# A third token tile of 128 rows in a one-core hybrid layer (mLSTM, SSD, ConvFFN), FFN constant rows read at another time, and another order of the first transfers

## The chip, the core and the metric

The kernel runs on one core of one Trainium2 chip. The metric is the device time of one execution in microseconds (us); the kernel before is given as three runs with their median, and one further execution was profiled. Engines are called by the profile's names: PE (matmul), PEld (its weight load), DVE, ACT, POOL and SP. SP issues nearly all of the transfers; POOL and ACT issue some.

## What is computed

One layer of a decoder, in f32, for 256 prompt tokens (one sequence, states start at zero) and 64 sample tokens (8 sequences of 8 tokens, each with states of its own):

```
u = x @ w_in                                   # 2048 -> q, k, v, o, gates, z, xbc, dt
h_m = mLSTM(q, k, v, gates)                    # 4 heads of 256; per sequence a carried C, n, m
h_s = SSD(z, conv4(xbc), dt)                   # 16 heads of 64, 2 groups; per sequence a carried S
x1 = LN1(alpha * x + [h_m, h_s] @ w_out)
up = x1 @ w_up                                 # 2048 -> 2 * 5504
c = conv3(up) ; f = (silu(c_g) * c_v) @ w_down
y = LN2(alpha * x1 + f)
```

Within a sequence of L tokens both mixers are a masked L x L product (the scores with their decays, times v) plus a carry-in: the state at the sequence's start, seen through q or C. The outputs are y for both token sets and every new state.

## The kernel before, in words

**Tokens and weights.** The 320 tokens (NT) lie in the free dimension of all large products: a bank holds 128 outputs x 320 tokens. f32 is kept by splitting both sides: x into XH and XL (rounded part and rest), each weight tile into hi and lo. Each tile of 128 x 128 weights takes three matmuls of 320 columns (XH·hi, XL·hi, XH·lo); there are 9456 of these, called main matmuls here. Class `Stream` brings the weights: raw blocks by DMA into a ring of 4 (L61), a quarter of 128 x 512 at a time rounded by ACT to hi (L74) and subtracted by DVE to lo (L75), into rings of 5.

**Stages.** w_in; w_out; then up and down projection in three parts; at the end LN2 (L1618 to L1661). `run_groups` (L262) walks through the weight groups. L232 is the helper that records every matmul, L238 the one for every transpose.

**The rest of the work** is written as generators: `yield n` puts the next piece n units later on a clock that the program keeps for itself while it is built, and pieces are put between main matmuls when they are due on it. So the yields fix, at build time, the order of each engine's instructions; each engine then works through its own order and waits for its inputs.

**Token tiles.** Where tokens must stand in partitions, they are taken as three tiles, two of 128 prompt tokens and one of the 64 samples (`tok(i)`: 128, 128, 64). That third tile gives matmuls and transposes with 64 rows:
- `x_transpose` (L402): x comes in as [tokens, features] and is transposed on PE, three transposes per 128 features, the third from a 64-row tile; ACT writes XH (L413), DVE XL (L414).
- `load_small` (L462): the constants; the SSD conv history is [24, 1536] and takes 12 transposes.
- `ssd_sample` makes the SSD carry-in `yi` of the samples, two tiles of [128, 512] per group in which each sequence has a block of 32 partitions (8 of them used). `ssd_heads` then adds, per pair of heads, masked products for the prompt and the samples; the carry-in comes in by two matmuls with `sel`, a constant that picks the used rows. In the same bank `po` is the prompt's state update.
- `ml_chunks` makes the mLSTM carry-in: per head two tiles of [128, 257], copied from PSUM by ACT (L1176). `ml_out` waits for both and for the products of the head, and for the samples adds one masked product (64 rows) and two matmuls with `sel` of 257 columns; num is then transposed with a 64-row third piece.
- `ssd_cb`, `ml_scores`, `colbc`, `ssd_norm`, `ln1`, `down_task` and the end treat the third tile likewise, with 64 rows or 64 columns.

**Around w_out.** In this stage `out_task` (L1373) follows each of 16 outputs of 128 x 320: DVE adds alpha·x (L1376) and takes a mean off (L1389), ACT rounds it (L1391), DVE takes the rest (L1393), ACT squares (L1402), and POOL adds both into running sums s1 (L1400) and s2 (L1403). For the first output POOL copies s1 instead (helper L193). Nobody waits for the sums before LN1. `ffn_consts` (L1339) runs beside it: after `yield 25000` POOL issues 8 transfers of `state_ffn_conv` rows (L1343), one of `ffn_conv_w` (L1345) and one of `ffn_conv_b` (L1346) into tiles called rows; after `yield 20000` PE transposes the four blocks of w and b, and DVE copies them to fcol (L1351); more transposes follow for the history (hist, L1357). The up projection needs them after LN1.

**Start.** PE runs 7 matmuls on ones. SP issues x_prompt's first columns, ident (the identity that transposes need), x_sample's first columns and more; ACT's queue issues the first two w_in blocks. POOL issues the small constants.

Of the kernel before, what the change touches and what calls it, by code (L numbers as in the profile page):

```python
# [13 lines left out]
NT = 320  # L14
# [7 lines left out]
class Stream:  # L22
# [21 lines left out]
    def load(self, upto=None, own=()):  # L44

        own = list(own)
        while self.nr < len(self.raws) and (own or self.live < self.RB):
# [12 lines left out]
            for c in range(0, m, step):  # L60
                (self.nc.sync if self.nr > 1 else self.nc.scalar).dma_start(t[:, :, c:c + step], src[:, :, c:c + step])  # L61
# [109 lines left out]
def _hybrid_step(ctx, tc, I, O):  # L171
# [77 lines left out]
    def tok(i):  # L249
        return 128 if i < 2 else 64  # L250
# [3 lines left out]
    sel = cp.tile([128, 2, 64], F32, name="sel")  # L254
# [58 lines left out]
    def diag3(dg, cols_of):  # L313
        for i in range(3):
            n = tok(i)
            V.tensor_scalar(dg[0:n, i, 0:n], ident[0:n, 0:n], cols_of(i)[0:n], None, ALU.mult)
        return dg

    def colbc(dg):

        ps = bank()
        for i in range(3):
            n = tok(i)
            mm(ps[:, 128 * i:128 * i + n], ones[0:n, :], dg[0:n, i, 0:n], True, True)
        return ps
# [63 lines left out]
    for _ in range(7):  # L389
# [12 lines left out]
    def x_transpose(c, kks=range(4)):  # L402
# [4 lines left out]
        for kk in kks:  # L407
# [27 lines left out]
    xs_in = mt("T10", [64, D])  # L435
    for c in range(4):
        x_load(c)
        s = slice(512 * c, 512 * c + 512)
        dma(xs_in[:, s], I["x_sample"].rearrange("b t f -> (b t) f")[:, s])
        if c == 0:  # L440
            src = I["x_prompt"][0, :, 256:512].rearrange("(i p) f -> p i f", p=128)
            dma(box["x", 0][:, :, 256:512], src)
            own = [mt("T4", [128, 1024]) for _ in range(4)]
        st.load(2 * c + 2, (own[0:2], own[2:4], (), ())[c])
# [16 lines left out]

    def load_small():  # L462
# [14 lines left out]
        hr = mt("T10", [24, 1536])  # L477
        gdma(hr, I["state_ssm_conv"][0].rearrange("b r c -> (b r) c"))
        gdma(c_tm, I["c_tm"])
        gdma(dsk, I["ssm_D"].broadcast_to([128, 16]))  # L480
        gdma(m01, I["c_m01"])
        gdma(sel, I["c_sel"])
# [5 lines left out]
        for i in range(12):  # L488
            transpose(ps[:, 24 * i:24 * i + 24], hr[:, 128 * i:128 * i + 128])
        A.activation(histx, ps[:, 0:288].rearrange("p (a b) -> p a b", b=24), AF.Copy)  # L490
# [20 lines left out]
    def gate_task(pg):  # L511
        gf, gi = mt("T2", [128, 384]), mt("T2", [4, NT])
        V.memset(gf[:, NT:384], 0.0)
        V.tensor_copy(gf[:, 0:NT], pg[:, 0:NT])
# [5 lines left out]
        for i in range(3):  # L520
            mm(pt[:, 24 * i:24 * i + 24], gf[:, 128 * i:128 * i + 128], fold[:, 0:24], True, True)
        pf = bank()
        mm(pf[0:4, 0:NT], fold[:, 0:4], gf[:, 0:NT], True, True)
# [36 lines left out]
        transpose(pd[0:48, 0:64], dt3[0:64, 2, :])  # L560
# [4 lines left out]
        V.tensor_copy(dtf[32:48], pd[32:48, 0:64])  # L565
# [47 lines left out]
        for i in range(3):  # L613
            transpose(p1[:, 128 * i:128 * i + 128], T1[:, 128 * i:128 * i + 128])
        A.activation(TT1, p1[:, 0:384].rearrange("p (a b) -> p a b", b=128), AF.Copy)
        p2 = bank()
# [59 lines left out]
    def ssd_cb():  # L676
# [4 lines left out]
        for g in range(2):  # L681
# [3 lines left out]
            mm(ps[0:64, 384:448], B[:, g, 256:NT], C[:, g, 256:NT], True, True)  # L685
            t = mt("T2", [128, 448])
            G.memset(t[64:128, 384:448], 0.0)
            V.tensor_tensor(t[:, 0:384], ps[:, 0:384], m01[:, 0:384], ALU.mult)
            V.tensor_tensor(t[0:64, 384:448], ps[0:64, 384:448], m01[0:64, 384:448], ALU.mult)
# [76 lines left out]
    def ssd_xdt():  # L766
# [3 lines left out]
        for i in range(3):  # L770
            n = tok(i)
            for hh in range(2):
                ps = bank()
                for j in range(4):
                    transpose(ps[0:n, 128 * j:128 * j + 128], XS[:, 4 * hh + j, 128 * i:128 * i + n])
                V.tensor_tensor(by(xdt[0:n, i, 512 * hh:512 * hh + 512], 64), by(ps[0:n, :], 64),
                                bcl(dt3[0:n, i, 32 + 8 * hh:40 + 8 * hh], 64), ALU.mult)
                yield 500
        box["xdt"] = xdt
        flags.add("xdt")  # L780

    def ssd_sample():
# [22 lines left out]
        yield from wait("x4")  # L805
        yi = {}
        for b in range(8):
# [19 lines left out]
            if b % 4 == 3:  # L827
                x = b // 4
                for g in range(2):
# [6 lines left out]
                    yi[g, x] = y  # L836
# [5 lines left out]
        box["yi"] = yi  # L842
# [5 lines left out]
    def ssd_heads():  # L848
# [41 lines left out]
        for j in range(8):  # L890
# [47 lines left out]
    def ssd_norm():  # L938
        var = sm([128, 3, 2])
        G.memset(var, 1.0)  # L940
        for g in range(2):
# [10 lines left out]
            for i in range(3):  # L952
                mm(ps[0:tok(i), 2 * i:2 * i + 2], sq[:, 128 * i:128 * i + tok(i)], ones[:, 0:2], True, True)
            pv = ps[:, 0:6].rearrange("p (a b) -> p a b", b=2)
            V.tensor_scalar(var[:, 0:2, g], pv[:, 0:2, 0], 1.0 / 512, None, ALU.mult)
            V.tensor_scalar(var[0:64, 2:3, g], ps[0:64, 4:5], 1.0 / 512, None, ALU.mult)
# [769 lines left out]
```

## Time and profile before

| what | value |
| --- | --- |
| three runs, median (lowest to highest) | 1579.27 us (1578.6 to 1581.3) |
| the profiled execution: its own time, its span | 1580.12 us, 1578.3 us |
| mean clock of PE in it, share of full | 0.992 |
| PE busy, share of the span | 98% |
| DVE, ACT, POOL busy | 62%, 49%, 18% |
| HBM traffic | 231.63 MB read, 20.43 MB written |

The span runs from the first to the last instruction of the profile; the execution's own time is 1.8 us longer. In rows of the timeline the first number is the start in us from the span's start, the second the length of the (merged) row, then engine, line, operation, output<-inputs by tile name, shape and count; in brackets the idle time ahead of it and what ended it. Matmuls overlap in the pipeline, so the price of one is read from start to start, not from its length. A row of the windows gives the stretch, its length, busy time and instruction count of PE, PEld, DVE, ACT and POOL, the granted clock, the busy share of the DMA engines and GB/s.

### The profile page before, as it was taken

The page shows a single profiled execution, that of the slowest core. Times are in us where ns is not written, and L with a number is a line of the kernel's source. Part 1 is how long each engine was busy: PE and PEld are TensorE (multiplying, and loading weights), DVE is VectorE, ACT ScalarE, POOL GpSimd, SP SyncE. Part 2 cuts the span into 40 slices and gives each one's busy share as a digit, 9 for nine tenths or more (in the row PEclk, how much of TensorE's full clock was granted, in tenths as well). Part 3 has the DMA queues.
Part 4 walks back from the last instruction along what each step waited for, and adds up shares of the span by engine and source line. Part 5 has one row for each costly group of instructions (what it writes and reads, how often), then busy time and mean ns, then how long its engine had stood idle before and what let it go on. Part 6 is the DMA issues. An engine that isn't in the chain of part 4 may idle for free.

```text
span 1578.3 us, 27987 instructions
## 1 busy us (share of the span) xinstructions
PE 1553.8 (98%) x10547; PEld 1502.5 (95%) x10547; DVE 976.6 (62%) x1957; ACT 773.1 (49%) x1532; POOL 290.3 (18%) x601
## 2 busy tenths in 40 slices
PE   9999999999999997999999999999999999999997
PEld 7999999998889997999999999999999999999996
DVE  5775445656677585687777545565644465556765
ACT  3665433435445453476666435555533455555332
POOL 4213220024311073133321000000000000001301
PEclk9999999999999998999999999999999999999998
DMA  9456665577665566445554455455444545455642
GB/s 260 147 161 160 187 187 172 143 193 208 195 221 183 169 183 138 134 147 149 149 151 135 157 158 146 148 156 152 136 152 144 167 145 151 143 154 168 170 140 79
DMA packets 267080, 253.97 MB, mean 161 GB/s; under 512 B 18804, under 2 KB 261263, under 8 KB 266816
## 3 DMA queue, kind: packets, MB, share of 16 engines
q1 hardware_dynamic: 260432, 246.76, 53.2%
q0 software_dynamic: 4928, 4.37, 1.3%
q8 instruction: 82, 1.34, 0.3%
q10 hardware_dynamic: 1584, 1.05, 0.3%
q14 instruction: 54, 0.44, 0.1%
HBM read 231.63 MB, written 20.43 MB: 160 GB/s over the span
## 4 chain that ended last, share of the span: by engine, by line
PE 86%; issue 7%; DMA 2%; POOL 1%; DVE 1%; ACT 1%; POOLq 0%; SPq 0%; DVEq 0%; ACTq 0%
PE bk L232 84%; PE bk L238 2%; DMA rows<-ffn_conv_w 1%; POOL T L425 1%; DMA raw<-w_out 1%; DVE lo L75 1%; DMA T<-ln_g 0%; DMA gbias<-ssm_dt_bias 0%; DMA xT<-T 0%; POOL big L1654 0%; ACT hi L74 0%; DVE big L1393 0%; DVE big L1389 0%; ACT L657 0%; ACT T L644 0%
## 5 line engine op out<-in xcount | busy, mean ns | idle before, releaser
L75 DVE TENSOR_TENSOR lo<-raw,hi 128x512 fp32r<-128x512 f32 (+2 forms) x800 | 556.4, 706 | 391.7 <-ACT hi L74 389.3
L74 ACT ACTIVATE hi<-raw 128x512 fp32r<-128x512 f32 (+2 forms) x800 | 486.3, 616 | 455.9 <-PE bk L232 427.3
L232 PE MATMUL bk<-big,hi 128*128 128x320 f32 (+1 forms) x2752 | 609.3, 310 | 0.0
L232 PEld LDWEIGHTS bk<-big,hi 128*128 128x128 f32 x2752 | 462.2, 188 | 0.1
L232 PE MATMUL bk<-big,lo 128*128 128x320 f32 (+1 forms) x1376 | 426.5, 310 | 0.0
L232 PE MATMUL bk<-XH,hi 128*128 128x320 f32 x832 | 270.2, 325 | 0.1
L232 PEld LDWEIGHTS bk<-big,lo 128*128 128x128 f32 x1376 | 259.3, 188 | 0.0
L232 PE MATMUL bk<-XH,lo 128*128 128x320 f32 x832 | 258.2, 310 | 0.1
L232 PE MATMUL bk<-XL,hi 128*128 128x320 f32 x832 | 258.0, 310 | 0.0
L232 PE MATMUL bk<-HH,hi 128*128 128x320 f32 x688 | 214.2, 311 | 0.0
L232 PE MATMUL bk<-HH,lo 128*128 128x320 f32 x688 | 212.6, 309 | 0.0
L232 PE MATMUL bk<-HL,hi 128*128 128x320 f32 x688 | 212.5, 309 | 0.0
L232 PEld LDWEIGHTS bk<-XH,hi 128*128 128x128 f32 x832 | 157.2, 189 | 14.7 <-issue 5.5
L232 PEld LDWEIGHTS bk<-XL,hi 128*128 128x128 f32 x832 | 157.4, 189 | 0.4
L232 PEld LDWEIGHTS bk<-XH,lo 128*128 128x128 f32 x832 | 157.2, 189 | 0.6 <-DVE lo L75 0.6
L1492 DVE SCALAR_TENSOR_TENSOR c<-c,fcol,c 128x336 f32<-128x336 f32 x172 | 98.0, 570 | 58.6 <-ACT c L1490 55.6
L232 PEld LDWEIGHTS bk<-HL,hi 128*128 128x128 f32 x688 | 129.2, 188 | 0.0
L232 PEld LDWEIGHTS bk<-HH,hi 128*128 128x128 f32 x688 | 129.2, 188 | 0.0
L232 PEld LDWEIGHTS bk<-HH,lo 128*128 128x128 f32 x688 | 129.1, 188 | 0.0
L193 POOL TENSOR_SCALAR fst<-c 128x18 f32<-128x18 f32 x86 | 22.2, 265 | 567.4 <-ACT c L1485 567.4
L232 PE MATMUL bk<-MH,hi 128*128 128x320 f32 x256 | 80.9, 316 | 0.0
L232 PE MATMUL bk<-MH,lo 128*128 128x320 f32 x256 | 80.1, 313 | 0.7 <-DVE lo L75 0.7
(338 smaller groups left out, 1505.8 us busy)
## 6 DMA issues: line engine op xcount, KB each, us to landing
raw<-ffn_w_up SPq DMA_DIRECT2D x172, 512.0 KB, 3.8
raw<-w_in SPq DMA_DIRECT2D x100, 512.0 KB, 4.1
raw<-ffn_w_down SPq DMA_DIRECT2D x71, 512.0 KB, 3.6
raw<-w_out SPq DMA_DIRECT2D x32, 512.0 KB, 3.9
T<-state_mlstm_C SPq DMA_DIRECT2D x32, 256.0 KB, 5.8
s_C<-T SPq DMA_DIRECT2D x32, 256.0 KB, 4.9
T<-state_ssm SPq DMA_DIRECT2D x8, 512.0 KB, 6.5
s_ssm<-T SPq DMA_DIRECT2D x8, 512.0 KB, 5.3
```

The lines of the kernel that those rows point to most:

```text
L74: nc.scalar.activation(h, src, AF.Copy)
L75: nc.vector.tensor_tensor(l, src, h.bitcast(F32), ALU.subtract)
L193: G.tensor_scalar(out, in_, 1.0, 0.0, ALU.mult, ALU.add)
L232: nc.tensor.matmul(out, lhsT=lhsT, rhs=rhs, start=start, stop=stop)
L238: nc.tensor.transpose(out, in_, ident[b:b + p, b:b + p])
L425: G.tensor_tensor(t, f32(XH(k, 2)), f32(XL(k, 2)), ALU.add)
L1492: V.scalar_tensor_tensor(c[:, 0:336], xp[:, j:j + 336], fcol[:, j, i:i + 1], c[:, 0:336], ALU.mult, ALU.add)
```

## The change

The third token tile becomes `TS[2] = slice(192, 320)`: the last 64 prompt tokens once more, and the 64 samples, which now stand in partitions 64 to 127. Transposes and products of the third tile thereby have 128 rows; of the repeated prompt tokens nothing is read, or their place is masked or overwritten.
- The low 64 partitions of the third tile carry the carry-in: `gather` (four DMAs on POOL's queue for each `yi` tile) moves the used rows of `yi` into the low half of xdt's (SSD) or VT's (mLSTM) third tile, and the mask's low half is an identity. One matmul of 128 rows then adds product and carry-in. `sel` and its matmuls are gone. There are 16 gather DMAs in `ssd_sample` (8 x 512 each) and 32 in `ml_chunks` (8 x 257 each); `ssd_sample` now waits for "xdt" too.
- `po` is written as two halves of 64 columns.
- x_sample comes in as [128, 1024], two column halves on top of each other: 8 transposes instead of 16, with ACT and DVE writing XH and XL in more pieces (24 pairs of instructions instead of 16). The conv history comes as [96, 384]: 3 transposes instead of 12. Some constants are loaded with their halves swapped (6 more DMAs on POOL's queue at the start, 2 more POOL transfers later, for the mLSTM mask).
- `ffn_consts`: the yields 25000 and 20000 become 12000 and 40000.
- First transfers: ident and the first x_sample columns on ACT's queue, w_in blocks 0 and 1 on SP's, another order behind them; 9 warm-up matmuls.

The diff, cut to its core:

```diff
+    TS = (slice(0, 128), slice(128, 256), slice(192, NT))
...
-                (self.nc.sync if self.nr > 1 else self.nc.scalar).dma_start(t[:, :, c:c + step], src[:, :, c:c + step])
+                self.nc.sync.dma_start(t[:, :, c:c + step], src[:, :, c:c + step])
...
-            mm(ps[:, 128 * i:128 * i + n], ones[0:n, :], dg[0:n, i, 0:n], True, True)
+            mm(ps[:, TS[i]], ones, dg[:, i, :], True, True)
+        mm(ps[:, 256:NT], ones, dg[:, 2, 64:128], True, True)
...
-            dma(ident, I["c_ident"])
+            nc.scalar.dma_start(ident, I["c_ident"])
...
-            transpose(ps[:, 256:NT], xs_in[:, 128 * k:128 * k + 128])
-            A.activation(XH(k), ps[:, 0:NT], AF.Copy)
-            V.tensor_tensor(XL(k), ps[:, 0:NT], f32(XH(k)), ALU.subtract)
+            parts = [(k, 0, 256)]
+            if k < 8:
+                transpose(ps[:, 256:384], xs_in[:, 128 * k:128 * k + 128])
+                parts = [(k, 0, NT), (k + 8, NT, 384)]
...
-        for i in range(12):
-            transpose(ps[:, 24 * i:24 * i + 24], hr[:, 128 * i:128 * i + 128])
+        for a in range(3):
+            transpose(ps[:, 96 * a:96 * a + 96], hr[:, 128 * a:128 * a + 128])
...
-            mm(ps[0:64, 384:448], B[:, g, 256:NT], C[:, g, 256:NT], True, True)
+            mm(ps[:, 384:448], B[:, g, TS[2]], C[:, g, 256:NT], True, True)
...
+    def gather(out, y):
+
+        for c in range(4):
+            gdma(out[8 * c:8 * c + 8], y[32 * c:32 * c + 8])
...
-        yield from wait("x4")
+        yield from wait("x4", "xdt")
...
-                    yi[g, x] = y
+                    gather(box["xdt"][32 * x:32 * x + 32, 2, 512 * g:512 * g + 512], y)
...
-            for x in range(2):
-                mm(ps[:, 256:NT], box["yi"][g, x][:, 128 * (j % 4):128 * (j % 4) + 128], sel[:, x, :], x == 0, False)
             for e, (p, f) in enumerate(pe):
-                mm(ps[p, 256:NT], xdt[0:64, 2, f], mw[e][0:64, 384:448], False, True)
+                mm(ps[p, 256:NT], xdt[:, 2, f], mw[e][:, 384:448], True, True)
             for i in range(2):
-                mm(po, xw[:, i, :], btok[:, i, g, :], i == 0, i == 1)
+                for e, (p, f) in enumerate(pe):
+                    mm(po[p, :], xw[:, i, p], btok[:, i, g, :], i == 0, i == 1)
...
-                box["yi", h, x] = yi
+                gather(box["VT"][32 * x:32 * x + 32, 2, h, 0:257], yi[:, 0:257])
...
-        mm(ps[0:64, 0:257], P[0:64, 384:448], VT[0:64, 2, h, 0:257], True, False)
-        for x in range(2):
-            mm(ps[0:64, 0:257], sel[:, x, :], box.pop(("yi", h, x))[:, 0:257], False, x == 1)
-        A.activation(num[0:64, 2, 0:257], ps[0:64, 0:257], AF.Copy)
+        mm(ps[:, 0:258], P[:, 384:512], VT[:, 2, h, :], True, True)
+        A.activation(num[:, 2, :], ps[:, 0:258], AF.Copy)
...
-            for i in range(3):
-                transpose(ps[:, 128 * i:128 * i + tok(i)], num[0:tok(i), i, 128 * e:128 * e + 128])
+            for i in (2, 0, 1):
+                transpose(ps[:, TS[i]], num[:, i, 128 * e:128 * e + 128])
...
     def ffn_consts():
-        yield 25000
+        yield 12000
         hr = fr("rows", [86, 16, 128])
...
-        yield 20000
+        yield 40000
         ps = bank()
         for j in range(4):
             transpose(ps[:, 86 * j:86 * j + 86], wr[:, j, :])
```

Two places show how the change moves instructions. The first is POOL's order in the w_out stage. Before, the ten transfers of FFN rows stand behind twelve of the sum additions (c is s1 or s2, the third name the square; the pcopy of s1 stands ahead of these rows):

```order
L1400 TENSOR_TENSOR c_6271<-c_6271,big_6268 128x320
L1403 TENSOR_TENSOR c_6272<-c_6272,c_6624 128x320
L1400 TENSOR_TENSOR c_6271<-c_6271,big_6268 128x320
L1403 TENSOR_TENSOR c_6272<-c_6272,c_6629 128x320
L1343 DMA rows_6636<-state_ffn_conv 86x2x128 x8
L1345 DMA rows_6645<-ffn_conv_w 86x3x128
L1346 DMA rows_6645<-ffn_conv_b 86x128
L1400 TENSOR_TENSOR c_6271<-c_6271,big_6268 128x320
L1403 TENSOR_TENSOR c_6272<-c_6272,c_6668 128x320
```

In the changed kernel they stand directly behind the pcopy (L193), and the twelve additions (L1426 and L1429 there) come behind them:

```order
L193 TENSOR_SCALAR c_6323<-big_6320 128x320
L1369 DMA rows_6502<-state_ffn_conv 86x2x128 x8
L1371 DMA rows_6511<-ffn_conv_w 86x3x128
L1372 DMA rows_6511<-ffn_conv_b 86x128
L1426 TENSOR_TENSOR c_6323<-c_6323,big_6320 128x320
L1429 TENSOR_TENSOR c_6324<-c_6324,c_6534 128x320
L1426 TENSOR_TENSOR c_6323<-c_6323,big_6320 128x320
L1429 TENSOR_TENSOR c_6324<-c_6324,c_6576 128x320
```

So the transfers move ahead of twelve additions, and the additions behind ten issues. On PE the transposes of w and b move the other way: they stand behind main matmul 3048 before and behind 3096 now, 48 main matmuls later.

The second place is one pair of SSD heads on PE, between two main matmuls (bk is the pair's bank; T the mixer's operands: xdt with the decayed masks, then xw with the B tokens):

```order
L232 MATMUL bk_2964<-T_240_2829,T_156_1738 64x256
L232 MATMUL bk_2964<-T_241_2834,T_156_1738 64x256
L232 MATMUL bk_2964<-T_240_2829,T_156_1738 64x128
L232 MATMUL bk_2964<-T_241_2834,T_156_1738 64x128
L232 MATMUL bk_2964<-sel,T_202_2288 128x64
L232 MATMUL bk_2964<-sel,T_233_2733 128x64
L232 MATMUL bk_2964<-T_240_2829,T_156_1738 64x64
L232 MATMUL bk_2964<-T_241_2834,T_156_1738 64x64
L232 MATMUL bk_2964<-T_149_1720,T_242_2839 128x128 x2
```

The same pair in the changed kernel:

```order
L232 MATMUL bk_2988<-T_240_2853,T_156_1730 64x256
L232 MATMUL bk_2988<-T_241_2858,T_156_1730 64x256
L232 MATMUL bk_2988<-T_240_2853,T_156_1730 64x128
L232 MATMUL bk_2988<-T_241_2858,T_156_1730 64x128
L232 MATMUL bk_2988<-T_240_2853,T_156_1730 64x64
L232 MATMUL bk_2988<-T_241_2858,T_156_1730 64x64
L232 MATMUL bk_2988<-T_149_1712,T_242_2863 64x128 x4
```

The two matmuls with sel are gone, and the last two are four of half the columns. There are eight such pairs. The trace counts each of these small f32 matmuls twice or more (its rows show, for instance, x4 where the order has two).

More of the change, by code (lines that the diff above doesn't have):

```diff
@@ L314, in diag3 @@
         for i in range(3):
-            n = tok(i)
-            V.tensor_scalar(dg[0:n, i, 0:n], ident[0:n, 0:n], cols_of(i)[0:n], None, ALU.mult)
+            V.tensor_scalar(dg[:, i, :], ident, cols_of(i), None, ALU.mult)
         return dg
@@ L321, in colbc @@
         ps = bank()
[L322 to L324 removed]
+        for i in range(2):
+            mm(ps[:, TS[i]], ones, dg[:, i, :], True, True)
+        mm(ps[:, 256:NT], ones, dg[:, 2, 64:128], True, True)
         return ps
@@ L388, in _hybrid_step @@
     warm = bank()
-    for _ in range(7):
+    for _ in range(9):
         mm(warm[:, 0:128], ones, ones, True, True)
@@ L411, in x_transpose @@
                 transpose(ps[:, 128 * i:128 * i + 128], t[:, i, 128 * kk:128 * kk + 128])
-            transpose(ps[:, 256:NT], xs_in[:, 128 * k:128 * k + 128])
-            A.activation(XH(k), ps[:, 0:NT], AF.Copy)
-            V.tensor_tensor(XL(k), ps[:, 0:NT], f32(XH(k)), ALU.subtract)
+            parts = [(k, 0, 256)]
+            if k < 8:
+                transpose(ps[:, 256:384], xs_in[:, 128 * k:128 * k + 128])
+                parts = [(k, 0, NT), (k + 8, NT, 384)]
+            parts = [(kx, slice(256 if a else 0, 256 if b == 256 else NT), ps[:, a:b]) for kx, a, b in parts]
+            for kx, o, src in parts:
+                A.activation(XH(kx)[:, o], src, AF.Copy)
+            for kx, o, src in parts:
+                V.tensor_tensor(XL(kx)[:, o], src, f32(XH(kx))[:, o], ALU.subtract)
     def keep_x():
@@ L433, in keep_x, with xs_load @@
         yield from gate_task(pg)
[L435 to L444, printed above, removed]
+    xs_in = mt("T10", [128, 1024])
+    xs_src = I["x_sample"].rearrange("b t f -> (b t) f")
+    def xs_load(eng, a, b):
+        for e in range(2):
+            eng.dma_start(xs_in[64 * e:64 * e + 64, a:b], xs_src[:, 1024 * e + a:1024 * e + b])
+    x_load(0)
+    xs_load(nc.scalar, 0, 256)
+    own = [mt("T4", [128, 1024]) for _ in range(4)]
+    st.load(1, own[0:1])
+    dma(box["x", 0][:, :, 256:512], I["x_prompt"][0, :, 256:512].rearrange("(i p) f -> p i f", p=128))
+    xs_load(nc.sync, 256, 512)
+    st.load(2, own[1:2])
+    x_load(1)
+    st.load(3, own[2:3])
+    xs_load(nc.sync, 512, 1024)
+    st.load(4, own[3:4])
+    x_load(2)
+    st.load(6)
+    x_load(3)
+    st.load(8)
     gw = mt("T2", [128, 16, 32])
@@ L460, in _hybrid_step, with swapped @@
     n0f = sm([128, 64], name="n0f")
+    def swapped(out, in_):
+        for e in range(2):
+            gdma(out[64 * e:64 * e + 64], in_[64 - 64 * e:128 - 64 * e])
     def load_small():
@@ L476, in load_small @@
         gdma(m0, I["state_mlstm_m"][0].rearrange("b h -> h b"))
-        hr = mt("T10", [24, 1536])
-        gdma(hr, I["state_ssm_conv"][0].rearrange("b r c -> (b r) c"))
-        gdma(c_tm, I["c_tm"])
+        hr = mt("T2", [96, 384])
+        for q in range(4):
+            gdma(hr[24 * q:24 * q + 24], I["state_ssm_conv"][0].rearrange("b r c -> (b r) c")[:, 384 * q:384 * q + 384])
+        swapped(c_tm[:, 2, :], I["c_tm"][:, 2, :])
+        gdma(c_tm[:, 0:2, :], I["c_tm"][:, 0:2, :])
         gdma(dsk, I["ssm_D"].broadcast_to([128, 16]))
-        gdma(m01, I["c_m01"])
-        gdma(sel, I["c_sel"])
+        gdma(m01[:, 0:384], I["c_m01"][:, 0:384])
+        swapped(m01[:, 384:448], I["c_m01"][:, 384:448])
         yield 17000
@@ L684, in ssd_cb @@
             mm(ps[:, 256:384], B[:, g, 128:256], C[:, g, 128:256], True, True)
-            mm(ps[0:64, 384:448], B[:, g, 256:NT], C[:, g, 256:NT], True, True)
+            mm(ps[:, 384:448], B[:, g, TS[2]], C[:, g, 256:NT], True, True)
             t = mt("T2", [128, 448])
-            G.memset(t[64:128, 384:448], 0.0)
+            pcopy(t[0:64, 384:448], ident[0:64, 0:64])
             V.tensor_tensor(t[:, 0:384], ps[:, 0:384], m01[:, 0:384], ALU.mult)
-            V.tensor_tensor(t[0:64, 384:448], ps[0:64, 384:448], m01[0:64, 384:448], ALU.mult)
+            V.tensor_tensor(t[64:128, 384:448], ps[64:128, 384:448], m01[64:128, 384:448], ALU.mult)
             cbm.append(t)
@@ L770, in ssd_xdt @@
         for i in range(3):
-            n = tok(i)
+            p = slice(64 * (i == 2), 128)
             for hh in range(2):
@@ L952, in ssd_norm @@
             for i in range(3):
[L953 to L956, printed above, removed]
+                mm(ps[:, 2 * i:2 * i + 2], sq[:, TS[i]], ones[:, 0:2], True, True)
+            V.tensor_scalar(var[:, :, g], ps[:, 0:6].rearrange("p (a b) -> p a b", b=2)[:, :, 0], 1.0 / 512, None, ALU.mult)
             yield 0
@@ L1211, in ml_out @@
         num = mt("T4", [128, 3, 258])
-        G.memset(num[64:128, 2, :], 1.0)
         ps = bank()
@@ L1532, in down_task @@
         if j == 2 and m == 15:
-            for i in range(3):
-                t = slice(128 * i, 128 * i + tok(i))
+            for t in (slice(0, 128), slice(128, NT)):
                 V.tensor_tensor(a[:, t], a[:, t], ps[:, t], ALU.add)
@@ L1636, in _hybrid_step @@
     for i in range(3):
-        transpose(ps[0:5, 128 * i:128 * i + tok(i)], f32(nbc[0:tok(i), i, :]))
+        transpose(ps[0:5, 128 * i:128 * i + 128], f32(nbc[:, i, :]))
     for i in range(3):
-        t = slice(128 * i, 128 * i + tok(i))
+        t = slice(128 * i, 128 * i + 128)
         V.tensor_copy(nbr[:, t], ps[0:5, t])
```

91 lines of the change are left out of this document (42 added, 49 removed).

## The prediction, made before the changed kernel ran

> **What bounds the kernel now.** I read the page first: busy shares and clock.
>
> ```profile
> span 1578.3 us, 27987 instructions
> PE 1553.8 (98%) x10547; PEld 1502.5 (95%) x10547; DVE 976.6 (62%) x1957; ACT 773.1 (49%) x1532; POOL 290.3 (18%) x601
> PEclk9999999999999998999999999999999999999998
> ```
>
> PE has work in 98% of the span, at full clock but for two slices; DVE, the next, is at 62%. So time can only come from PE's own instructions or from the few places where it stands. A stretch of PE's timeline in the FFN gives the price of a main matmul:
>
> ```profile
> 899.74 0.31 PE L232 MATMUL bk<-HL,hi 128*128 128x320 f32 x1
> ...
> 901.94 0.31 PE L232 MATMUL bk<-HL,hi 128*128 128x320 f32 x1
> ```
>
> Fifteen matmuls in 2.20 us: 0.147 us each, whatever the rows' own 0.31 says. 9456 of them are 1390 us, and the change leaves these as they are. The rest, some 190 us, is small matmuls, transposes and idle time. The waits of PE, and then the windows around the longest of them:
>
> ```profile
> PE bk L238 <- DMA rows<-ffn_conv_w: 8.3, 1, 8.3
> PE bk L232 <- DVE lo L75: 0.7, 1, 0.7
> ```
>
> ```profile
> 593.50:602.00 8.50, 0.33 (x3) 0.06 (x1) 3.55 (x2) 0.63 (x1) 3.00 (x4) 0.71 1.22 197
> 602.00:607.20 5.20, 5.11 (x21) 5.11 (x22) 2.04 (x5) 0.63 (x1) 0.00 (x0) 0.50 0.17 56
> 570.00:580.00 10.00, 10.00 (x70) 10.00 (x69) 9.76 (x17) 5.52 (x12) 7.02 (x7) 1.00 0.37 105
> ```
>
> PE stands from 593.5 to 602.0 for the FFN's rows (busy 0.33 of 8.50), and then runs 5.2 us at a granted clock of 0.50. The place costs 8.2 idle and half of 5.2: **10.8 us**. The third window is the same stage a little earlier: there DVE is busy for 9.76 of 10 us.
>
> **Part 1: the FFN rows begun sooner, transposed later.** POOL's timeline:
>
> ```profile
> 551.81 0.46 POOL L193 TENSOR_SCALAR c<-big 128x320 f32<-128x320 f32 x1 [36.45 <-DMA raw<-w_out]
> ...
> 576.06 12.80 POOL L1343 DMA_DIRECT2D rows<-state_ffn_conv  x8
> 588.85 1.84 POOL L1345 DMA_DIRECT2D rows<-ffn_conv_w  x1
> 590.69 0.56 POOL L1346 DMA_DIRECT2D rows<-ffn_conv_b  x1
> 591.27 0.76 POOL L1400 TENSOR_TENSOR c<-c,big 128x320 f32<-128x320 f32 x1
> ...
> 595.65 0.85 POOL L1403 TENSOR_TENSOR c<-c,c 128x320 f32<-128x320 f32 x1
> ```
>
> Issuing takes 12.80 + 1.84 + 0.56 = 15.2 us. Behind the pcopy it runs from 552.3 to 567.5 on the old time axis; the slowest landing is that of ffn_conv_w (the transfers of 590 to 600):
>
> ```profile
> rows<-ffn_conv_w POOLq DMA_DIRECT2D x1, 129.0 KB, 13.2
> ```
>
> So all rows are there by about 581. PE's transposes come 48 main matmuls (7.1 us) later than the 593.5 at which it stood, at 600.6. The margin is some 20 us: the wait goes, and the half clock behind it. Reading later costs nothing by itself: the up projection that needs these constants comes behind LN1.
>
> What it moves: twelve additions now queue behind 15.2 us of issues and start at 567.5 instead of 556. Nobody waits for the sums before LN1. But they then run back to back, and that has a price on DVE. Its timeline beside the six additions from 591.27 to 596.50:
>
> ```profile
> 588.14 0.69 DVE L75 TENSOR_TENSOR lo<-raw,hi 128x512 fp32r<-128x512 f32 x1 [1.14 <-ACT hi L74]
> ...
> 592.21 4.85 DVE L75 TENSOR_TENSOR lo<-raw,hi 128x512 fp32r<-128x512 f32 x2 [2.22 <-ACT hi L74]
> ```
>
> Two lo subtractions take 4.85 us instead of 1.38: 3.5 us lost to six additions, 0.58 each. Today nobody sees it, PE stands then anyway. Twelve in a row cost DVE up to 7 us between 567 and 580, just where it has 0.24 us to spare; of this it loses a part already, since the twelve lie among its work there now. Bounds for PE: 0 (hi and lo are made ahead, rings of 5) and 5 us (7 less what is lost now). I take 2.5: walking through the new order of DVE and POOL with these prices, the lo's come some 3.5 us later than now, and about 1 us of lead covers that. The rows also meet the w_out blocks and rx on the DMA engines, as at 593 (share 1.22), but the blocks' ring of four holds some 14 us of PE work (a block is 24 main matmuls); 0. Net gain of part 1: 10.8 - 2.5 = **8.3 us**.
>
> **Part 2: the third tile of 128 rows.** Prices on PE. A group of x transposes (four times two full tiles and one of 64 rows), and four plain full ones:
>
> ```profile
> 19.02 2.30 PE L238 MATMUL bk<-ident,T 128*128 128x128 f32 x12
> 21.25 0.41 PE L232 MATMUL bk<-XH,hi 128*128 128x320 f32 x1
> ```
>
> ```profile
> 143.91 0.60 PE L238 MATMUL bk<-ident,T 128*128 128x128 f32 x4
> 144.27 0.39 PE L232 MATMUL bk<-XH,hi 128*128 128x320 f32 x1
> ```
>
> Start to start: 2.23 us for twelve against 0.36 for four, so 0.19 against 0.09 to 0.10 each. A 64-row piece lengthens its group of three from 0.27 to 0.56: **0.29 us** each. The Trainium skill, TensorEngine Tiling (Array Packing), Theoretical Speedup, says that up to 64 rows or columns give up to twice the speed; by that alone the pieces' 8.9 us below (3.9, 2.3 and 2.7) would not be there, and the time would be 1557. Its Key Properties add that changing the tiling mode drains TensorE, and the rows agree with that side: the piece is dearer than a full tile.
> - x: the group of quarter 1 keeps twelve transposes (2.23 to 1.2), those of quarters 2 and 3 keep eight (2.23 to 0.8): 1.0 + 1.4 + 1.4 = 3.9 with rounding. (Quarter 0: part 3.) ACT and DVE write 24 pieces for 16; both are under 62%, so 0.
> - num: 8 pieces at 0.29: 2.3. History: 9 transposes fewer at 0.09: 0.8.
> - ssd_cb 2, scores 4, colbc 4, sums 4: 14 pieces that no quoted row prices. Bounds 0 and 0.29; I take 0.19, since some stand among other narrow work: 2.7 (0 to 4.1).
>
> A pair of SSD heads:
>
> ```profile
> 254.51 0.87 PE L232 MATMUL bk<-T,T 128*64 128x256 f32 x8
> 255.31 0.66 PE L232 MATMUL bk<-sel,T 128*128 128x64 f32 x4
> 255.90 0.97 PE L232 MATMUL bk<-T,T 64*64 64x64 f32 x8
> 256.62 0.39 PE L232 MATMUL bk<-XH,hi 128*128 128x320 f32 x1
> ```
>
> sel's part goes: 0.59 (255.31 to 255.90). po's full matmuls become pairs of half columns, as the first row's, where eight take 0.80: some 0.17 less. Together 0.76, eight times: **6.1**. The mLSTM's third product, and the price of full ones of 258 columns:
>
> ```profile
> 387.30 0.65 PE L232 MATMUL bk<-T,T 64*64 64x257 f32 x2
> 387.87 1.08 PE L232 MATMUL bk<-T,sel 128*64 128x257 f32 x4
> 388.88 0.42 PE L232 MATMUL bk<-XH,hi 128*128 128x320 f32 x1
> ```
>
> ```profile
> 348.42 1.47 PE L232 MATMUL bk<-T,T 128*128 128x258 f32 x6
> 349.54 0.50 PE L232 MATMUL bk<-XH,hi 128*128 128x320 f32 x1
> ```
>
> 1.58 us now; one product after, which the trace counts twice, so 2 x 0.19 at most and 0.2 at least. I take 0.22, as the six end in a slow next matmul: 1.36, four times **5.4**. Sum of part 2: 3.9 + 2.3 + 0.8 + 2.7 + 6.1 + 5.4 = **21.2 us**.
>
> What it adds: 48 gather transfers. The second carry-in tile of a head is written by ACT, and its reader on PE:
>
> ```profile
> 408.82 0.46 ACT L1176 ACTIVATE T<-bk,TT 128x257 f32<-128x257 f32 x1
> ```
>
> ```profile
> 421.25 1.08 PE L232 MATMUL bk<-T,sel 128*64 128x257 f32 x4
> ```
>
> 12.0 us lie between the two. Four issues at 0.56 (ffn_conv_b above) are 2.2; small transfers on POOL's queue landed in
>
> ```profile
> p_n<-sm POOLq DMA_DIRECT2D x1, 4.0 KB, 4.8
> ```
>
> so 7.0 us of 12.0: hidden. The SSD's gathers stand 108 main matmuls (15.9 us) ahead of their reader. Behind a gather POOL's copies and its products for the SSD queue for 2.2 us; PE reads both later than that, and POOL is at 18%. Its six extra transfers at the start are behind nothing that PE reads soon. 0 for all of these, if the landing stays like this (third rival).
>
> **Part 3: the start.** PE's first steps:
>
> ```profile
> 7.42 1.27 PE L238 MATMUL bk<-ident,T 64*128 64x64 f32 x4 [1.29 <-DMA T<-x_sample]
> 8.83 0.64 PE L232 MATMUL bk<-XH,hi 128*128 128x320 f32 x1
> ```
>
> x_sample's first columns move from third place on SP's queue to second on ACT's: the 1.29 goes, and quarter 0 has four 64-row pieces less at 0.29 or, at half clock, more: 1.3. Together 2.6; bounds 0 (w_in's first block, now behind others on SP, is the last to come) and 4.
>
> **Sum.** 8.3 + 21.2 + 2.6, less 0.6 for places where lo is only just in time (the 0.7 wait above): 31.5 us. The profiled execution took 1580.1 (span 1578.3 and 1.8 around it), so 1548.6; the median of the runs is 0.8 lower: **1548 us**.
>
> **Rivals.**
> 1. *The additions starve DVE* (0.10). Twelve in a row hold DVE for most of 10 us, and PE stands for 6 to 7 us beyond lo's lead, with half clock behind it. For it: the 4.85 us row. Against: in the window from 570 POOL is busy for 7.02 of 10 us, and DVE still does all of its work. Part 1 then brings 1 instead of 8.3: 1555 us. The Trainium skill, SBUF — State Buffer, section on the two separate sides, speaks against the change here: a DVE operation with two SBUF inputs and a GpSimd operation that reads SBUF lock each other out of a shared pair of ports, whole instructions at a time. By that rule, the row agrees: 2.4 us per lo beside additions.
> 2. *PE's savings are given back as waits for hi and lo* (0.08), in the heads above all, where PE is to be 0.76 faster every pair: the 6.1 are lost, 1554 us. Against: PE waits for lo once in the whole run, 0.7 us, and DVE is at 62%.
> 3. *The gathers land late* (0.04), the slower side. By the dearest rows, 1.6 per issue (12.80 / 8) and 13.2 to land, the low half of VT is there after 19.6 us, 7.6 us behind its reader; with 2.6 of half clock some 9 to 10 us, four times: 1548 + 38 = 1586 us. It decides when the four waits exceed 31.5 us, 7.9 each. Against: those rows were 129 KB in rows of 512 bytes beside full DMA engines; these are 8 rows each.
> 4. *The change doesn't do what it says: the rows still come too late* (0.03), as the transfers spread over more than the 20 us of margin among full DMA engines. Part 1 brings nothing: 1556 us. Against: 13.2 us was the landing with the engines full.
>
> **How the numbers follow.** The forecast has 0.75. Its low end: no new wait (3.1 more), the start at 4, the 14 pieces at 0.29 (1.4 more): 1542, and 1 for what the shares of one execution leave open: 1541. High: the two rivals at 1554 and 1555, or the start and the 14 pieces at 0 with a stall of 5: 1556, and 2 for a gather that is late now and then: 1558. About 0.2% (3.2 us) is what a measurement of this kernel tells from no change. Faster by more: all but the third rival, 0.95; within it 0.01; slower 0.04.
>
> **What would show it.** Right: PE's wait for ffn_conv_w gone and PEclk full in its slice; POOL's issues right behind the pcopy; no row with sel; about 0.2 us for the third mLSTM product; the first main matmul at 6 to 7.5 us. Wrong: PE waiting for lo L75 around 560 to 575 (first rival), in every pair of heads (second), or for VT or xdt by a POOL transfer (third).

## The result and the profile after

The changed kernel takes 1559.34 us (median of 4 runs, 1558.87 to 1560.59); the kernel before, in runs beside it, 1579.24 (1578.6 to 1581.3). The ratio is 0.9873, with an interval of 0.9856 to 0.989: 19.9 us faster. The forecast was 31.5 us. Its direction holds; the time lies 1.3 us above the top of its range. The profiled execution took 1559.26 us. Its page and its list of PE's waits (us in total, times, longest):

```profile
span 1557.5 us, 28098 instructions
PE 1532.4 (98%) x10518; PEld 1494.8 (96%) x10518; DVE 977.9 (63%) x1959; ACT 773.5 (50%) x1540; POOL 320.3 (21%) x661
```

```profile
PE bk L232 <- DVE lo L75: 4.3, 3, 1.9
PE bk L232 <- DMA T<-w_in: 3.9, 1, 3.9
PE bk L238 <- DMA T<-x_sample: 1.3, 1, 1.3
PE bk L232 <- ACT hi L74: 1.0, 1, 1.0
PE bk L238 <- DVE XL L418: 0.5, 1, 0.5
```

The wait for ffn_conv_w is gone, as forecast. Two others are there that the list of before did not have at this size: lo (0.7 before), and a piece of w_in. x_sample's 1.3 has not gone either, and 1.0 for hi (at 8.6) and 0.5 for XL (at 41.1) are new.

Both traces hold all 9456 main matmuls, so the start of the N-th one in each is a common clock. The lead of a kernel at main matmul N is by how many us it starts that one sooner than the kernel before, each counted from its own span's start. What the changed kernel gains between marks of that clock, beside the terms of the forecast that belong there:

| main matmuls | lead gained, us | forecast | what was to come here |
| --- | --- | --- | --- |
| start to 320 | 0.25 | 7.3 | start 2.6, x 3.9, history 0.8 |
| 320 to 2560 | 15.79 | 16.5 | heads 6.1, third product 5.4, num 2.3, the 14 pieces 2.7 |
| 2560 to 2944 | -5.43 | -2.5 | additions beside DVE |
| 2944 to 3088 | 11.47 | 10.8 | wait for the FFN rows |
| 3088 to the end | -1.24 | -0.6 | places where lo is just in time, forecast without a place |
| sum | 20.84 | 31.5 | |

These are the two profiled executions, 20.8 us apart; the medians are 19.9 apart. Two lines carry the miss: the first, by 7.1, and the third, by 2.9.

**The first line.** The lead grows to 4.25 us at main matmul 84, where the forecast's terms give 5.0 (start 2.6, two x groups 1.0 and 1.4), and is -1.20 at 108. Between them lies the first matmul of the gates (f32, 32 outputs, from a tile called T). Before, on PE:

```profile
32.33 0.31 PE L232 MATMUL bk<-XH,lo 128*128 128x320 f32 x1
32.57 0.75 PE L232 MATMUL bk<-T,T 128*32 128x320 f32 x8
```

And after, the same two:

```profile
28.06 0.31 PE L232 MATMUL bk<-XH,lo 128*128 128x320 f32 x1
32.26 0.78 PE L232 MATMUL bk<-T,T 128*32 128x320 f32 x8 [3.89 <-DMA T<-w_in]
```

PE is there 4.3 us sooner and stands 3.9 us. The tile T (gw in the code) is brought by SP in two transfers of narrow columns of w_in. The second one's issue in the SP timeline, before and then after:

```profile
21.14 7.80 SPq L450 DMA_DIRECT2D T<-w_in  x1
```

```profile
22.08 7.03 SPq L467 DMA_DIRECT2D T<-w_in  x1
```

By the view of DMA issues it lands 10.9 us behind the start of its issue before, 10.0 after: at 32.0 and 32.1. The matmul started at 32.57 and 32.26. So before, PE came to the gates half a microsecond behind a transfer that nobody saw; the change saved time on PE ahead of a landing that did not move with it. Then comes half clock, as the windows of the changed kernel show for the stretch of the wait and the 4 us behind it:

```profile
28.00:32.30 4.30, 0.41 (x7) 0.17 (x8) 1.84 (x4) 0.63 (x1) 0.00 (x0) 1.00 0.69 94
32.30:36.30 4.00, 4.00 (x20) 3.45 (x21) 0.00 (x0) 0.00 (x0) 0.00 (x0) 0.57 0.97 305
```

**The third line.** POOL after, in the w_out stage:

```profile
536.17 12.71 POOL L1369 DMA_DIRECT2D rows<-state_ffn_conv  x8 [0.16 <-issue]
548.88 1.84 POOL L1371 DMA_DIRECT2D rows<-ffn_conv_w  x1
...
551.31 0.76 POOL L1426 TENSOR_TENSOR c<-c,big 128x320 f32<-128x320 f32 x1
...
558.59 0.85 POOL L1426 TENSOR_TENSOR c<-c,big 128x320 f32<-128x320 f32 x1
```

Issues and additions stand as forecast; nine additions run without a gap from 551.31 to 559.4. DVE beside them:

```profile
551.44 1.18 DVE L75 TENSOR_TENSOR lo<-raw,hi 128x512 fp32r<-128x512 f32 x1 [1.15 <-ACT hi L74]
...
553.06 4.13 DVE L1415 TENSOR_TENSOR big<-big,c 128x320 f32<-128x320 f32 x2
557.11 2.68 DVE L1419 SCALAR_TENSOR_TENSOR big<-big,cols,big 128x320 fp32r<-128x320 f32 x1
559.71 0.68 DVE L75 TENSOR_TENSOR lo<-raw,hi 128x512 fp32r<-128x512 f32 x1
```

The row of 4.13 merges two operations, and a view that cuts the first one off shows that the second has nearly all of it:

```profile
553.64 3.55 DVE L1415 TENSOR_TENSOR big<-big,c 128x320 f32<-128x320 f32 x1
```

So 8.3 us lie between the starts of two lo's (551.44 and 559.71); between the same two in the kernel before it is 4.1 (566.45 to 570.58). PE waits for the second, and once more 7 us later:

```profile
560.45 0.41 PE L232 MATMUL bk<-MH,lo 128*128 128x320 f32 x1 [1.94 <-DVE lo L75]
567.40 0.42 PE L232 MATMUL bk<-MH,lo 128*128 128x320 f32 x1 [1.64 <-DVE lo L75]
```

(The third wait of the list, 0.7, is at 531.85, as one of 0.7 was before.) And the windows there:

```profile
558.00:562.00 4.00, 2.06 (x14) 1.80 (x13) 3.96 (x6) 0.95 (x3) 1.44 (x2) 0.99 0.28 67
562.00:566.00 4.00, 3.76 (x16) 3.50 (x14) 3.93 (x7) 3.71 (x8) 3.58 (x5) 0.59 0.33 110
```

DVE is full (3.96 and 3.93 of 4), PE does half of the first window, and has a clock of 0.59 in the second. The one wait of 1.94 ahead of it is short, but the clock falls all the same. By the lead, the first wait costs 2.1 us, the half clock 1.5 and the second wait 1.8; the stretch costs 5.6 with what lies between, where 2.5 was forecast.

### The profile page after: what moved, and what is told of

It reads as the page before. It is cut to its first block, busy times and chain, and to the rows that moved or that the text cites. A ratio compares the mean times of both kernels' runs of the same rounds, so it can differ in the third digit from the quotient of the medians.

```text
span 1557.5 us, 28098 instructions
## 1 busy us (share of the span) xinstructions
PE 1532.4 (98%) x10518; PEld 1494.8 (96%) x10518; DVE 977.9 (63%) x1959; ACT 773.5 (50%) x1540; POOL 320.3 (21%) x661
## 4 chain that ended last, share of the span: by engine, by line
PE 95%; DMA 2%; DVE 2%; SPq 1%; POOL 0%; issue 0%; ACT 0%; POOLq 0%; DVEq 0%; ACTq 0%
PE bk L232 92%; PE bk L238 2%; DMA T<-w_in 1%; DMA raw<-w_out 1%; SPq L61 0%; DVE lo L75 0%; DVE big L1415 0%; POOL big L1674 0%; DVE big L1419 0%; DMA ident<-c_ident 0%; SPq L466 0%; SPq L394 0%; DVE big L1402 0%; DVE big L1432 0%; DVE big L1676 0%
## 5 line engine op out<-in xcount | busy, mean ns | idle before, releaser
L193 POOL TENSOR_SCALAR fst<-c 128x18 f32<-128x18 f32 x86 | 22.0, 263 | 567.6 <-ACT c L1508 567.6
```

The source lines that it names most:

```text
L193: G.tensor_scalar(out, in_, 1.0, 0.0, ALU.mult, ALU.add)
```

## The experiments

In the texts below, quarters 243 to 245 are the hi and lo around main matmul 2920. Theory A: the additions, made one burst by the moved issues, hold DVE, and the delay costs PE some 5.6 us. Theory B, its rival: what costs there is the rows' traffic on the DMA engines beside w_out's blocks, or late hi. Theory C: the gate tile's landing swallows the start's gains; its rival, that the reordered first transfers only move the delay. Each median stands beside runs of the kernel before on the same chip, which had medians between 1578.85 and 1579.36. Ratios are to these. Where "one execution" is said there is no ratio, and the trace is read.

**1. The FFN yields alone, in the kernel before.**

```diff
-        yield 25000
+        yield 12000
...
-        yield 20000
+        yield 40000
```

> The kernel before with nothing changed but the two yields of ffn_consts (12000 and 40000). Both theories see the same two sides here: the wait for ffn_conv_w and its half clock go (11.5 us between main matmuls 3040 and 3088 in the changed kernel), and new waits for lo come 150 main matmuls earlier (5.6 us there). Expected: 1579.2 - 11.5 + 5.6 = 1573.3 us. If the early issue were worth its full price without a new wait (a third possibility: the waits of the changed kernel come from its other parts), 1568.

Measured: 1575.56 us (1574.19 to 1577.98), ratio 0.9977 [0.9967, 0.9987]. In its profile 6.6 us are lost between main matmuls 2850 and 3040 and 11.5 won at 3088. PE's waits there:

```profile
PE bk L232 <- DVE lo L75: 4.6, 2, 3.1
```

So both sides of part 1 are there without the rest of the change: the wait for the rows is worth what was forecast, and most of it is paid to the additions. The median is 2.3 us above the expected number.

This trace also bears on theory C. Its start is that of the kernel before, and yet it leads that kernel's trace by 0.95 us at main matmul 84, so two executions of one start differ by about 1 us. At 108 the lead is 0.07, and between lies a wait that the kernel before does not show:

```profile
PE bk L232 <- DMA T<-w_in: 0.8, 1, 0.8
```

**2. The change with the old yields** (25000 and 20000).

> The changed kernel with the two yields of ffn_consts as before (25000 and 20000). Theory A (twelve additions in a row on POOL hold DVE's operations) and theory B (the rows' transfers make the w_out blocks late) both put the new waits with the early issue, so both give 1559.3 + 11.5 - 5.6 = 1565.2 us, with PE waiting 8 us for ffn_conv_w and not for lo around main matmul 2920. If the waits for lo came from the other parts of the change, they stay: 1570.

Measured: 1563.05 us (1562.73 to 1567.17), ratio 0.99 [0.9886, 0.9915]. The loss at the additions goes (5.6 us of lead against the changed kernel by main matmul 2944), and the wait is back:

```profile
PE bk L238 <- DMA rows<-ffn_conv_w: 8.1, 1, 8.1
```

The median is 2.2 below the expected number. Part 1 is worth 3.7 us in medians here, 3.3 in the first experiment; 8.3 was forecast. By the leads at main matmul 3088 the two sides leave 6.1 here and 4.9 there. The execution profiled here took 1567.17, 4.1 above the median, and why the traces give more than the medians is open.

**3. The changed kernel without the twelve additions.** The LN1 sums lack six of the sixteen outputs.

```diff
-            e.tensor_tensor(s1, s1, d, ALU.add)
+            if m > 6:
+                e.tensor_tensor(s1, s1, d, ALU.add)
```

The same for s2.

> The changed kernel without the additions to s1 and s2 for outputs 1 to 6 (twelve; LN1's sums lack these outputs), all transfers as they are. Theory A: no operation of DVE beside 553 to 568 us takes over 1 us, no wait for lo there, 5.6 us less than the changed kernel: 1554. Theory B: the transfers alone make the waits: 1559, with lo's waits as they are.

Measured: 1556.19 us, one execution. PE's lead over the kernel before is 13.52 us all through the place, none is lost. The same windows:

```profile
558.00:562.00 4.00, 4.00 (x30) 4.00 (x29) 3.56 (x8) 2.19 (x6) 1.44 (x2) 1.00 1.08 188
```

The transfers of the rows run as before, and ACT waits 3.9 us in two places for w_out blocks, more than the 1.7 in the changed kernel. Theory B falls, A stands: it is the additions. (The total is short of the 5.6 because rx, an input of the stage, came late in this execution and cost 2.6 ahead of the place. That left DVE some time more; experiment 4 has no such delay.)

**4. Memsets of the same length in place of the twelve additions.** They write an unused tile and read nothing; the sums lack the same outputs.

```diff
+            else:
+                G.memset(scr[:, 0:896], 0.0)
```

> The changed kernel with the twelve additions of outputs 1 to 6 replaced by twelve memsets of about the same length on a tile that nobody reads (LN1's sums lack these outputs). It splits theory A: if any work of POOL in a row holds DVE, the waits for lo stay at about 5 us, the time at 1558 to 1559; if it is the additions' reads of SBUF that hold DVE's two-input operations, DVE runs freely beside memsets, and the waits go as without the additions: 1554 to 1556.

Measured: 1552.96 us, one execution; nothing lost at the place (lead 16.7 us throughout). POOL is as full as before, and DVE runs:

```profile
550.84 0.86 POOL L1430 MEMSET scr<- 128x896 f32 x1
...
560.83 0.85 POOL L1436 MEMSET scr<- 128x896 f32 x1
```

```profile
551.29 0.90 DVE L1416 TENSOR_TENSOR big<-big,c 128x320 f32<-128x320 f32 x2
552.10 0.55 DVE L1420 SCALAR_TENSOR_TENSOR big<-big,cols,big 128x320 fp32r<-128x320 f32 x1
...
555.62 0.66 DVE L1439 CAST big<-cols 128x16 fp32r<-128x16 f32 x1
```

0.90 and 0.55 us for what took 4.13 and 2.68; they run at that length while a memset runs (550.84 to 551.70, then 551.76 to 552.61), and between the same two lo's lie 3.0 us (549.57 to 552.56) and not 8.3. So it is not POOL's being busy that holds DVE's two-input operations but what the additions do and a memset does not, which is reading SBUF. The Trainium skill, SBUF — State Buffer, section "Who interferes with whom", says just this: a VectorE instruction with two SBUF inputs contends with a GpSimd instruction that reads SBUF, not with one that only writes. The CAST has one input and is longer beside memsets too: 0.66, against 0.17 in the run without additions. The time is 1 us below the expected range, of which one execution says little.

**5. The rows' issues spread among the additions** (a yield of 1500 behind each of the eight, then 25000).

> The changed kernel with the ten transfers of rows spread among the additions (a yield of 1500 behind each of the first eight, then 25000), so that the same bytes flow, over some 20 us, and no more than a pair or two of additions waits on POOL at a time. Theory A: DVE is not held for long, the waits for lo (5.6 us with their half clock) shrink to 1 or less: 1554 to 1555 us. Theory B: the same bytes beside the same w_out blocks, so most of the waits stay: 1558 us or more.

Measured: 1559.16 us (1556.27 to 1561.04), ratio 0.987 [0.9853, 0.9887]: the same as the changed kernel. In the trace 3.9 us are lost instead of 5.6, since the additions still come in twos and fours; one CAST of 16 columns takes

```profile
561.41 2.52 DVE L1433 CAST big<-cols 128x16 fp32r<-128x16 f32 x1
```

beside four of them. Theory A's number was missed, and the medians can't tell the two kernels apart.

**6. The same spread, and the rows issued by SP** (`gdma` to `dma` in the three statements). POOL then has additions alone.

> The changed kernel with the ten transfers of FFN rows on SP's queue instead of POOL's (spread by the yields of the run before, between the w_out blocks): POOL issues none of them, so its additions run as they come. Theory A (additions in a row hold DVE): the waits for lo go from 5.6 to under 1 us: 1554. Theory B (the transfers themselves make hi and lo late): they stay, or grow, since w_out's blocks now queue behind the rows on the same engine: 1559 or more.

Measured: 1557.96 us (1557.18 to 1558.78), ratio 0.9865 [0.9852, 0.9879]. The place of the additions loses 0.26 us instead of 5.64, but a new wait follows some 80 main matmuls behind (at 3024):

```profile
PE bk L232 <- ACT hi L74: 2.7, 2, 2.0
```

The rows, now ahead of w_out's blocks on SP's queue, delay them: ACT waits for raw blocks in three places there, 5.6 us in the longest, and hi comes late. The burst's cost goes; half of it comes back as the rival said, and the median lies between the two expected numbers. Behind the wait of 2.0 the clock does not fall in this trace:

```profile
577.60:581.00 3.40, 3.21 (x20) 2.96 (x21) 3.21 (x5) 3.40 (x8) 2.48 (x3) 1.00 0.90 335
```

**7. The gate tile's transfers sooner.** gw's memset and its two transfers stand behind `st.load(4, ...)`, ahead of the third x quarter.

```diff
+    gw = mt("T2", [128, 16, 32])
+    G.memset(gw[:, :, 24:32], 0.0)
     ...
     x_load(2)
     st.load(6)
```

> The changed kernel with the two transfers of the gate weights (gw, the narrow columns of w_in) moved forward on SP's queue, to behind w_in block 4 and ahead of x_prompt's third quarter. Theory C: all that PE gained by main matmul 90 (4.3 us) was lost again because the gate's matmul behind main matmul 96 waits for gw, which lands at 32 us in both kernels, and the idle time brings half clock. Then the wait of 3.9 us at 28 us goes, with the 1.5 us of half clock behind it: 1559.3 - 5.4 = 1554 us. Rival: the start is bounded by bytes, all transfers together, and what gw gains the w_in blocks or x's quarters lose; then PE waits for these instead and the time stays at 1558 to 1560.

Measured: 1556.74 us (1555.94 to 1559.54), ratio 0.9861 [0.9847, 0.9874]. SP issues them at 8.6 and 9.2 now, they land 9.7 and 12.3 us later, by 21.5, and the gates are begun without a wait for them:

```profile
28.61 0.31 PE L232 MATMUL bk<-XH,lo 128*128 128x320 f32 x1
29.36 0.75 PE L232 MATMUL bk<-T,T 128*32 128x320 f32 x8 [0.44 <-issue]
```

The lead over the changed kernel is 4.4 us from main matmul 120 on; 2.6 of it remain in the medians. In the trace the stretch 1696 to 2560 gains 1.1 less (PE waits 0.9 there for a T of DVE) and the additions take 6.6 instead of 5.6. The median lies between the expected 1554 and the rival's 1558 to 1560, but PE waits for no w_in block and no x quarter instead. Theory C stands. Of the 7.1 missing at the start, 4.4 are shown to be this tile's.

**8. Both: gates sooner, rows spread and on SP's queue.**

> Both of these edits together: the rows on SP's queue and gw early. If theories A and C hold and the two places are independent, the sum of both gains: 1559.3 - 5.4 - 5.0 = 1549 us, which is what the prediction's sum would be with its two missed waits gone. If either rival holds, 1553 to 1555.

Measured: **1554.00 us** (1553.25 to 1556.53), ratio 0.9843 [0.9829, 0.9856]: 5.3 us below the changed kernel and the fastest version whose sums are whole, but in the rivals' range (1553 to 1555) and not at 1549. hi's wait stays:

```profile
PE bk L232 <- ACT hi L74: 2.6, 2, 1.6
PE bk L232 <- issue: 1.2, 1, 1.2
```

3.8 us are lost between main matmuls 2970 and 3040.

**9. The same with the rows on ACT's queue** (`nc.scalar.dma_start`).

> As the run before (gw early, rows spread), but the ten transfers of rows on ACT's queue instead of SP's. With SP's queue PE's wait for lo at quarter 245 was gone, and PE waited 2.6 us for hi some 50 main matmuls later, since the w_out blocks came late behind the rows. Theory A plus a queue of their own for the rows: that wait shrinks too, 1554 - 3 = 1551 us. Rival (B, what is left of it): the DMA engines are shared whatever the queue, the blocks come as late, and ACT pays some 0.5 us per issue on top: 1554 to 1556.

Measured: 1561.46 us (1560.13 to 1562.19), ratio 0.9886 [0.987, 0.9903]: 7.5 us slower than the version with SP. ACT's own queue and its work:

```profile
559.95 4.75 ACTq L1373 DMA_DIRECT2D rows<-ffn_conv_b  x1
564.80 0.63 ACT L74 ACTIVATE hi<-raw 128x512 fp32r<-128x512 f32 x1 [5.43 <-issue]
```

The ten issues take 0.50 to 4.75 us each on ACT, and hi, which PE waits for (4.8 us in the longest wait), stands behind them. Some 9 us of lead go between main matmuls 2760 and 2970. Both numbers of the expectation were missed.

**10. The rows first, in POOL's idle time** (yields 6000 and 46000), issued from 504 to 519 by the span's clock, ahead of the outputs.

> The changed kernel with the two yields of ffn_consts at 6000 and 46000: POOL's ten issues now stand ahead of its pcopy, which waits 36 us for the first output of w_out, so they run in that idle time (from about 500 us), ahead of rx's transfers, and the additions find POOL free. Theory A: no additions in a row, no wait for lo at quarters 243 to 245, 5.6 us less: 1553.7. Theory B: the rows meet the w_out blocks there as well, lo's lead of 1.4 to 6 us is used up, and PE waits around 500 to 520 instead: 1557 or more.

Measured: 1560.82 us (1560.57 to 1561.89), ratio 0.9887 [0.9871, 0.9904]. No burst (0.26 lost there), but rx, the residual that DVE needs for each output, is now late:

```profile
DVE big L1402 <- DMA rx<-xT: 11.8, 1, 11.8
PE bk L232 <- issue: 4.8, 1, 4.8
```

PE stands about 5 us up to 534.5, ahead of a matmul that reads big, and 6.5 us of lead go between main matmuls 2700 and 2760. Theory A's number was missed; the time fits theory B's (1557 or more), but not its place: PE doesn't wait between 500 and 520. It is a third effect, rx, that neither theory named.

**11. The same with the gates sooner.**

> The same with gw early as well. Theories A and C: 1559.3 - 5.6 - 4.4 = 1549.3 us, the prediction's figure with both missed waits gone. If gw's early place costs later what it gained (its own run came out at 1556.7, with 1.8 us more of waits at quarters 243 to 245, where additions still ran in a row), 1551 or more.

Measured: 1556.31 us (1555.49 to 1556.76), ratio 0.9856 [0.9841, 0.9871]. The gates again bring 4.6 of lead over the changed kernel at main matmul 120, rx's wait stays (5.7 lost), and the 1549.3 of theories A and C was missed by 7.0; the time fits the rival's 1551 or more, but through rx.

**12. po in one piece of 128 columns, in the changed kernel.**

```diff
-                for e, (p, f) in enumerate(pe):
-                    mm(po[p, :], xw[:, i, p], btok[:, i, g, :], i == 0, i == 1)
+                mm(po, xw[:, i, :], btok[:, i, g, :], i == 0, i == 1)
```

> The changed kernel with po, the state update in each pair of SSD heads, as full matmuls again (two of 128 columns instead of four of 64). The prediction priced the split at 0.17 us less per pair, 8 pairs: PE loses 1.4 us over the heads (main matmuls 1264 to 1696), where it now gains 5.9 over the kernel before. Rival: the pairs of half columns cost as much as full ones (no overlap), and all of the 5.9 is sel's: 0 here.

Measured: 1559.87 us, one execution. One pair of heads, first with po whole, then in the changed kernel:

```profile
252.91 1.63 PE L232 MATMUL bk<-T,T 128*64 128x256 f32 x16
254.29 0.39 PE L232 MATMUL bk<-XH,hi 128*128 128x320 f32 x1
```

```profile
253.32 1.43 PE L232 MATMUL bk<-T,T 128*64 128x256 f32 x20
254.68 0.42 PE L232 MATMUL bk<-XH,hi 128*128 128x320 f32 x1
```

1.38 and 1.36 us from start to start, against 2.11 before. Over eight pairs the heads gain 5.89 us here and 5.95 in the changed kernel: splitting po brings 0.06, as the rival said.

## Why the prediction was right in direction and wrong in size

- **What bounds the kernel:** right. PE is busy in 98% before and after, and every gain and loss was read off PE's own order.
- **Heads, 6.1:** 5.95 measured, but the two parts were wrong and made up for each other. sel's going, with products of 128 rows in place of 64, is worth some 0.74 a pair and not 0.59, the split of po nothing instead of 0.17. That term was taken from another matmul's rows; experiment 12 shows it.
- **Third product 5.4, num 2.3, the 14 pieces 2.7:** sound in sum (the stretch from 320 to 2560, heads included, 15.8 of 16.5). The third product is 0.25 from start to start, 0.22 forecast:

```profile
379.85 0.60 PE L232 MATMUL bk<-T,T 128*128 128x258 f32 x2
380.10 0.50 PE L232 MATMUL bk<-XH,hi 128*128 128x320 f32 x1
```

So a 64-row piece among full tiles was rightly priced as dearer than a full tile. The time of 1557 that the prediction worked out from the Trainium skill's rule (TensorEngine Tiling (Array Packing), Theoretical Speedup) lies close to what was measured, but for another reason: the pieces' gains appear in the trace, and are lost elsewhere.
- **x, history and start, 7.3:** the step failed. The x groups got faster (a group of quarter 1 takes 1.23 us from start to start, 2.23 before), but the sum counted PE's work as if nothing on PE's way had a time of its own. gw's landing at 32 us had, 0.5 us ahead of its reader: 5.45 of lead go between main matmuls 84 and 108. No rival named it; the list of waits of before could not show it, for a transfer that lands just in time makes no wait. The four traces with that tile sooner (experiments 7, 8, 9 and 11) lose 0.5 to 1.6 between 84 and 120, those of the changed start with it in its old place 3.5 to 6.1; in experiments 7 and 11, 4.4 and 4.6 us come back against the changed kernel. The rest of the gap: 0.9 is missing by the first 20 main matmuls, where x_sample's wait of 1.3 stayed and hi's of 1.0 is new, and two executions of one start differ as much (experiment 1). 0.7 is missing at quarter 3's x group, which brings 0.7 and not 1.4; PE waits there 0.5 for XL, which DVE writes, and the prediction had put the writing of XH and XL at 0. Some 1.0 is not taken apart.
- **The wait for the rows, 10.8:** 11.5; right, and the half clock behind it was rightly counted.
- **The additions, 2.5:** 5.6, mis-sized. The mechanism was in the text, and the first rival had its form; PE lost 3.1 us more than forecast, where the rival had 7.3 more (part 1 bringing 1 instead of 8.3). The mean price of 0.58 us per addition held about: beside the burst of nine, three operations took 6.8 us instead of the 1.45 beside memsets, and a lo 0.5 more than usual, some 0.65 for each addition. What failed is the step from DVE's delay to PE's loss. Nearly all of it fell between two lo's, which came 4.1 us further apart than before (3.5 forecast), and the 2.5 held waiting alone. PE waited 1.9 and 1.6, and the half clock, at nothing in this term, took 1.5. The upper bound of 5 was too low: the traces with the burst whole (the changed kernel and experiments 1, 7 and 12) lose 5.6 to 6.6.
- **Gathers hidden, 0:** right. No wait for VT or xdt by a POOL transfer stands in the list, and the stretch that holds their readers gains its 15.8.
- **Behind main matmul 3088:** 1.2 us are lost, against 0.6 that the forecast spread over the run without a place. 1.1 of it lies behind the start of the last main matmul; the cause was not tested.

## What to carry to other kernels

A DMA issue that is moved on an engine moves everything behind it, and what was spread before may then come as one burst: look at which other engine's operations that burst makes longer. A saving of PE time ahead of a transfer that does not land sooner with it is no saving, so for each tile that comes by DMA compare its landing with its reader's start, where no wait is shown as well. And the rows found no free place: behind the additions PE waits for them, ahead of them DVE is held, on SP's queue w_out's blocks come late, on ACT's hi does, and ahead of everything rx does; what decided was how little each collision cost, and only runs told that.

## What the runs showed of the hardware that was not expected

- Additions that follow on POOL without a gap let a waiting DVE operation stand through about three of them: 3.55 us for one that takes 0.49, and 2.68 for one that takes 0.55, beside additions of 0.85 to 0.99. The Trainium skill's page SBUF — State Buffer, section "SBUF: two separate sides", says that the one that starts first holds the pair for its whole instruction. If the operation that waits had its turn next, that rule would cost it at most the rest of one addition; here one lost 3.1 us and one 2.1.
- A wait need not be long to halve the clock. The one wait ahead of it is of 1.94 us, and the granted clock falls to 0.5 from 561.9 to 565.3, 3.4 us, as behind the gates' wait (32.84 to 36.25). It is not sure to: in experiment 6 a wait of 1.96 (up to 577.62) was followed by none. The Trainium skill, TensorE: Matmul & The Clock Gate, Part 1, gives windows of about 3.4 us, and the lengths agree.
- An issue on ACT's queue took 0.50 to 4.75 us (experiment 9), and the rounding to hi stood for it, 5.4 us in the longest case.
